# Three blocks of 43 rows instead of four of 32 in the triangular solve of a gated DeltaNet layer, and other work at the kernel's start and end

## The chip, the cores and the metric

The kernel runs on one core of a Trainium2 chip. The core has five engines that each follow their own list of instructions: TensorE (PE, products), VectorE (DVE), ScalarE (ACT), GpSimd (POOL) and SyncE (SP), which here only issues DMAs. A loading of weights into the array is recorded apart, as PEld. Counted is the device time of one execution in microseconds. Three runs took 2796.86, 2797.15 and 2800.05 us, the median is 2797.15.

## The reference

256 tokens of width 2048 pass through two layers, all in f32. Layer 0 mixes tokens with a gated DeltaNet, layer 1 with a sparse attention; behind each mixer stand a layer norm, a gated feed-forward part with a short convolution (width 5120), another layer norm, and `x + sigmoid(x Wg) * (p Wp)`. The change is in layer 0 and in the very last sigmoid product. Of layer 0 this matters:

```python
def gated_delta_rule(q, k, v, g, beta):        # 32 heads of 128, q and k shared by two
    gc = jnp.cumsum(g, axis=-1)
    kb = k * beta[..., None]
    vb = v * beta[..., None]
    ...
    decay = jnp.where(tri, jnp.exp(jnp.where(tri, diff, 0.0)), 0.0)
    lmat = jnp.where(strict, jnp.einsum('bhncd,bhnsd->bhncs', kb, k) * decay, 0.0)
    amat = lmat + jnp.eye(C, dtype=jnp.float32)
    rhs = jnp.concatenate([vb, kb * jnp.exp(gc)[..., None]], axis=-1)
    sol = lax.linalg.triangular_solve(amat, rhs, left_side=True, lower=True, unit_diagonal=True)
```

`proj = x @ w_in` gives q, k, v, a gate z and the decays; q, k and v go through a causal convolution of four taps and a silu. The kernel cuts the 256 tokens into two halves of 128 (called a = 0 and 1), so each head needs the solution of two unit lower triangular systems of 128 rows, and the second one's right side depends on the first's solution.

## The kernel before

**Products.** Nearly all of the time goes into products with the weights in f32 precision. `weights()` (L101) fetches a raw tile of 512 KB (128 x 1024 f32) on SP's queue (L109), ScalarE rounds it into a high part `hi` (L114), and VectorE makes the rest `lo` (L115). Four raw tiles and three pairs of hi and lo exist. x stands transposed on chip as xT, also as a high and a low part. `gemm_t_steps` then makes 8 products of 128 x 512 with hi (L147: both parts of x at once) and 8 of 128 x 256 with lo (L151) per tile; `gemm_steps` does it with x as the stationary side (L184, L187, L190). In `gemm_steps` the last tile is done for one half of the tokens and then for the other, so that the first half's result can be used earlier.

**Groups.** Layer 0's 32 heads go by 8 groups of 4. For a group, `keys(g)` makes k and q (8 tiles, with convolution), `zgate` the gate z (8 tiles), `values` v (8 tiles, with convolution). The loop in `gdn_groups` writes them down as: values(g), then keys(g+1) and zgate(g+1), then `inverses`, `front(g+1)`, `substitute(g+1)`, `solve(g)`, `outputs(g)`. A scheduler turns this into one list per engine, by order of writing and by priorities; every engine and every DMA queue then works strictly in order.

**The solve.** A 128 x 128 triangular matrix is treated by blocks of rows on its diagonal, here four of 32:

- `front(g)`: `sums` makes the Gram products k k' on PE (g_ps, L542 and L543), `blocks` scales them into the strictly lower matrix L on VectorE (L574), SP stores the 32 x 32 diagonal blocks (lt, 4 DMAs, L579) and loads them again so that each partition of the chip has one whole block in a row (ld, 4 DMAs, L583).
- `substitute(g)`, on POOL: all 32 blocks of a group (2 halves, 4 heads, 4 blocks) are inverted at once by forward substitution. Block and column group share the 128 partitions: 32 blocks times 4 groups of columns, with 8 columns each. The start value xi (the identity) is copied from a constant, then come 31 steps of a multiply (L612) and a subtract (L614), each one step of a chain. At its end POOL stores xi (tt, 4 DMAs, L617).
- `inverses(g)`: POOL fetches the inverted blocks onto the diagonal of pm (4 DMAs, L631; pm is otherwise zero, and there is one pm). PE multiplies them with L (w_ps, through the helper `mul`, L623: four f32 products of 128 columns or fewer, one per head), and ScalarE copies what is above the block diagonal of the product into W.
- `solve(g)`: per half y0 = pm times the right side (s_ps<-vt,pm), then three times y = y0 - W y, a product on PE (s_ps<-y,W) and a subtract on VectorE (L691). With four blocks W is nilpotent of order four, so three rounds are exact. Between the halves stands the coupling product n21.

**POOL's queue** holds, in this order: pm fetches of group g, the substitution of group g+1 with its stores, and so on. **SP's queue** holds the weight tiles in the order in which PE uses them, with lt, ld and the decays' rows between them.

**The start.** `load(nb)` fetches four blocks of 512 columns of x (two DMAs each); PE transposes each (t_ps, 8 products by the identity, L231), and ScalarE and VectorE split it into xT (L224, L225). The first weight tiles stand between the blocks on SP's queue. Behind the transposes of block 1 POOL fetches the convolution's taps (128 KB) and a table of constants, cst (448 KB).

**The end.** `ple` makes the last product by blocks of 512 columns; for each half of a block ScalarE takes the sigmoid (L899), VectorE multiplies and adds (L900, L901), and SP stores the result (L903).

## Time and profile before

| What | us |
|---|---|
| median of the three runs | 2797.15 |
| the profiled execution | 2797.12 |
| its span, first to last instruction | 2795.1 |
| group loop of layer 0, one group to the next (stretch 138.8 to 224.2) | 85.4 |
| PE busy in that stretch | 85.35 |
| DVE, ACT, POOL busy in that stretch | 66.5, 48.7, 32.6 |
| first 30 us: PE busy | 22.4 |
| last 6.1 us: PE busy | 0.7 |

The granted clock of TensorE reads 1.00 in all stretches but the last. A table of stretches gives each engine's busy time in that stretch. A timeline row has the start, the duration, the engine, the line, the operation with output and inputs, the sizes, a count where equal rows were joined, and in brackets how long the engine stood idle before it and what ended that; SPq and POOL's DMA rows are the issuing of a DMA, not its transfer. A product's row of PE says "f32" also where the operands are the rounded parts. The profile's rows of products with f32 operands count each product twice, so x8 stands for four.

### The profile page before, as it was taken

Reading aid. Unit: us, or ns where it says so; the run is one execution under the profiler, and the core shown is the slowest. Engines: PE = TensorE matmul, PEld = TensorE weight load, DVE = VectorE, ACT = ScalarE, POOL = GpSimd, SP = SyncE. Lnnn points to the kernel's source line nnn. Section 1 sums busy time; section 2 is a strip of 40 time slices with the busy share of each in tenths; the row PEclk is TensorE's granted clock in tenths of the full one; section 3 lists DMA queues with packets and bytes.
Section 4 is the critical chain, followed back from the end, with each engine's and each line's share of the span. In section 5 each row is a group of like instructions: output and inputs, shape, how many; then the busy total and the mean of one; then the engine's idle time right before and its main releaser. Section 6 shows DMA issues by size and latency. Waiting matters only on the chain. (4 is left out here: it accounts for less than half of the span.)

```text
span 2795.1 us, 40216 instructions
## 1 busy us (share of the span) xinstructions
PE 2776.6 (99%) x14958; PEld 2390.1 (86%) x14958; DVE 1856.2 (66%) x3059; ACT 1421.6 (51%) x2239; POOL 337.7 (12%) x688
## 2 busy tenths in 40 slices
PE   8999999999999999999999999999999999999999
PEld 7888888888888888888888889888888888888887
DVE  6787787877556666666545665776676666655566
ACT  4555566555445555555434544455465555543453
POOL 1543234442200000000000000120000000000000
PEclk9999999999999999999999999999999999999999
DMA  7755665655565666666556567655556666665655
GB/s 213 205 157 158 166 176 164 168 152 159 173 210 164 193 206 206 207 196 207 196 191 208 171 198 215 181 152 163 181 181 196 197 187 199 194 195 195 207 171 195
DMA packets 412275, 520.82 MB, mean 186 GB/s; under 512 B 28940, under 2 KB 301712, under 8 KB 411824
## 3 DMA queue, kind: packets, MB, share of 16 engines
q1 hardware_dynamic: 404912, 499.91, 58.9%
q0 software_dynamic: 7168, 18.35, 2.7%
q8 instruction: 117, 1.92, 0.3%
q14 instruction: 78, 0.64, 0.1%
HBM read 513.94 MB, written 7.39 MB: 187 GB/s over the span
## 5 line engine op out<-in xcount | busy, mean ns | idle before, releaser
L115 DVE TENSOR_TENSOR lo<-raw,hi 128x1024 fp32r<-128x1024 f32 (+1 forms) x921 | 1125.0, 1223 | 606.0 <-ACT hi L114 594.6
L114 ACT ACTIVATE hi<-raw 128x1024 fp32r<-128x1024 f32 (+1 forms) x921 | 967.9, 1053 | 698.9 <-PE b_ps L187 469.5
L147 PE MATMUL mm_ps<-xT,hi 128*128 128x512 f32 (+1 forms) x4176 | 1027.9, 394 | 2.6 <-ACT hi L114 2.3
L147 PEld LDWEIGHTS mm_ps<-xT,hi 128*128 128x128 f32 (+1 forms) x4176 | 762.0, 188 | 148.9 <-ACT hi L114 2.9
L151 PEld LDWEIGHTS mm_ps<-xT,lo 128*128 128x128 f32 (+1 forms) x4176 | 539.4, 191 | 22.7 <-DVE lo L115 1.5
L151 PE MATMUL mm_ps<-xT,lo 128*128 128x256 f32 (+1 forms) x4176 | 557.2, 284 | 0.4 <-DVE lo L115 0.4
L184 PE MATMUL b_ps<-hi,xT 128*128 128x512 f32 (+1 forms) x704 | 270.9, 386 | 0.0
L187 PE MATMUL b_ps<-hi,xT 128*128 128x512 f32 (+1 forms) x704 | 268.8, 383 | 0.0
L220 ACT ACTIVATE fold<-mm_ps 128x256 f32<-128x256 f32 x261 | 98.1, 376 | 268.1 <-PE mm_ps L147 267.8
L184 PE MATMUL b_ps<-hi,hTA 128*128 128x512 f32 x512 | 199.3, 389 | 0.0
L187 PE MATMUL b_ps<-hi,hTA 128*128 128x512 f32 x512 | 199.2, 389 | 0.0
L190 PE MATMUL b_ps<-lo,xT 128*128 128x512 f32 (+1 forms) x704 | 188.4, 383 | 0.0
L239 POOL DMA_DIRECT2D lng<-in_ln_g x16 | 8.8, 547 | 1239.1 <-PE b_ps L190 654.5
L612 POOL TENSOR_TENSOR xt<-ld,xi 128x60 f32<-128x60 f32 (+24 forms) x248 | 116.2, 468 | 345.1 <-DMA ld<-lt 326.3
L187 PEld LDWEIGHTS b_ps<-hi,xT 128*128 128x128 f32 x704 | 132.2, 188 | 24.8
L184 PEld LDWEIGHTS b_ps<-hi,xT 128*128 128x128 f32 x704 | 132.2, 188 | 24.1
L190 PEld LDWEIGHTS b_ps<-lo,xT 128*128 128x128 f32 x704 | 129.9, 188 | 24.5
L190 PE MATMUL b_ps<-lo,hTA 128*128 128x512 f32 x512 | 136.8, 389 | 0.0
L190 PEld LDWEIGHTS b_ps<-lo,hTA 128*128 128x128 f32 x512 | 96.1, 188 | 20.0
L184 PEld LDWEIGHTS b_ps<-hi,hTA 128*128 128x128 f32 x512 | 96.1, 188 | 20.0
L187 PEld LDWEIGHTS b_ps<-hi,hTA 128*128 128x128 f32 x512 | 96.1, 188 | 19.9
L614 POOL TENSOR_TENSOR xi<-xi,xt 128x60 f32<-128x60 f32 (+24 forms) x248 | 107.5, 433 | 19.4
(266 smaller groups left out, 2571.0 us busy)
## 6 DMA issues: line engine op xcount, KB each, us to landing
raw<-in_gdn_w_in SPq DMA_DIRECT2D x193, 512.0 KB, 4.4
raw<-in_ffn_w_gate SPq DMA_DIRECT2D x160, 512.0 KB, 4.4
raw<-in_ffn_w_up SPq DMA_DIRECT2D x160, 512.0 KB, 4.6
raw<-in_ffn_w_down SPq DMA_DIRECT2D x160, 512.0 KB, 4.1
raw<-in_dsa_w_in SPq DMA_DIRECT2D x72, 512.0 KB, 3.7
raw<-in_gdn_w_o SPq DMA_DIRECT2D x64, 512.0 KB, 4.0
raw<-in_ple_w_gate SPq DMA_DIRECT2D x64, 512.0 KB, 4.9
raw<-in_dsa_w_o SPq DMA_DIRECT2D x32, 512.0 KB, 3.9
```

Source lines behind the costliest of these rows:

```text
L114: act = nc.scalar.activation(hi, raw, AF.Copy)
L115: ins = nc.vector.tensor_tensor(lo, raw, hi.bitcast(F32), op=ALU.subtract)
L147: ins = nc.tensor.matmul(q[:m, :], hi[:, k, o:o + m], x[:, k0 + k].rearrange("p a b -> p (a b)"), start=k0 + k == 0, stop=last)
L151: ins = nc.tensor.matmul(q[:m, S:], lo[:, k, o:o + m], x[:, k0 + k, 0, :], start=False, stop=last)
L184: ins = nc.tensor.matmul(ps[a][:, :n], xh, hi, start=k == 0, stop=False)
L187: self.before = nc.tensor.matmul(ps[a][:, :n], xl, hi, start=False, stop=False)
L190: self.last = nc.tensor.matmul(ps[a][:, :n], x(k)[:, 0, a * P:(a + 1) * P], lo, start=False, stop=k == kt - 1)
L220: nc.scalar.activation(t[:m], ps[:, S:], AF.Copy)
L239: ins = self.nc.gpsimd.dma_start(out=r, in_=bass.AP(tensor=src.tensor, offset=src.offset, ap=[[0, P], [1, n]]))
L612: nc.gpsimd.tensor_tensor(tmp[:, :m, :w], bcast(ld[:, i + 1:, i], m, 1), xi[:, :m, i:i + 1].to_broadcast([P, m, w]), op=ALU.mult)
L614: nc.gpsimd.tensor_tensor(xi[:, :m, i + 1:], xi[:, :m, i + 1:], tmp[:, :m, :w], op=ALU.subtract)
```

## The change

It has four parts.

1. **The solve by 43 rows.** The blocks are rows 0 to 41, 42 to 84 and 85 to 127 (42, 43 and 43 rows): three instead of four. `solve` does two rounds instead of three. The 24 blocks of a group still take 32 of the four times 32 places on the partitions, with 12 columns each. `substitute` has 42 steps; its start value xi is fetched by a DMA from the constants' table (264 KB, one buffer) instead of copied. ld becomes two tiles that exist once for all groups, the left 22 columns (43 x 22) and the right 21 (21 x 21); storing and loading them takes 6 + 8 DMAs (L634, L638) instead of 4 + 4. pm is fetched by 3 DMAs, w_ps has 86 columns, and W is copied in 2 pieces per half.
2. **Order around it.** `front(g+1)` without its last part is called behind the first tile of zgate(g+1) instead of behind `inverses(g)`, L gets two buffers, and the parts that need q (causal, squares, mixes) move into `values`. In group 0, front(1) and seven of the eight tiles of values(1) are called ahead of inverses(0).
3. **The start.** 13 products that nobody reads (idle_ps, on zeros in a part of xT that is written later) stand on PE ahead of and behind the first transposes. Block 0's transposes are split by pairs of columns (`begin`), the first weight tile is fetched and split by halves, a second weight tile is fetched ahead of block 1, the taps are fetched behind block 2, and the constants (now 256 KB without xi's start value) and ng behind block 3. The table of ones is a memset.
4. **The end.** The last block of 512 columns is done in three turns over its last two tiles: the second half's columns 0 to 255, the first half's all 512, the second half's columns 256 to 511; sigmoid, multiply, add and store follow by these pieces.

The diff, cut to its core:

```diff
+B_ROWS, B_COLS, B_LEFT = 43, 12, 22
+B_FROM = (0, 42, 85, P)
+N_CONST = C_XINIT + B_COLS * B_ROWS
...
+        parts = (slice(0, 2), slice(2, 4)) if self.fresh else (slice(0, nk),)
...
+            turns = [((0, 1), 0, n)] if not last else [((0,), 0, n), ((1,), 0, n)]
+            if last and fine:
+                turns = [((1,), 0, n // 2), turns[0], ((1,), n // 2, n // 2)]
...
+    def warm(self, n):
+
+        ps = self.mm.tile([P, 512], F32, tag="mm", name="idle_ps")
+        x = self.xT[:, KT - 1].rearrange("p a b -> p (a b)")
+        for _ in range(n):
+            self.nc.tensor.matmul(ps, x[:, :P], x, start=True, stop=True)
+
+    def begin(self, xT, x):
+
+        nc, out = self.nc, []
+        for k in (0, 2):
+            for a in range(2):
+                ps = self.sp.tile([P, 2, P], F32, tag="bk" if k else "sp", name="t_ps")
+                for j in (k, k + 1):
+                    self.turned = nc.tensor.transpose(ps[:, j - k], x[:, a, j * P:(j + 1) * P], self.ident)
+                out.append(self.split(xT[:, k:k + 2, 0, a * P:(a + 1) * P], xT[:, k:k + 2, 1, a * P:(a + 1) * P],
+                                      ps))
+        return [out[1], out[3]]
...
+                if nb:
+                    for a in range(2):
+                        self.halves = self.to_xT(self.xT, xs[nb][:, a], a, nb * 4, to)
+                    self.halves = [self.halves]
+                else:
+                    nc.vector.memset(self.xT[:, KT - 1].bitcast(F32), 0.0)
+                    self.warm(8)
+                    self.halves = self.begin(self.xT, xs[0])
+                    self.warm(5)
...
+                         2: [(cr, t["gdn_conv_w"].rearrange("k (n c) -> n k c", c=P))],
+                         3: [(self.cst, t["cst"][:, P:C_XINIT]),
                              (ng, t["gdn_norm_g"].rearrange("(p o) -> p o", o=1))]}.get(nb, ())
...
+        lds, nl = [], B_ROWS - B_LEFT
+        for k, n, o, tall in ((B_ROWS, B_LEFT, 0, 48), (nl, nl, B_LEFT, 32)):
+            lead = B_FROM[2] + o + tall - P
+            lt = self.dr.tile([32, lead + tall, n], F32, tag=f"lt{n}", name="lt", bufs=1)
+            ld = pool.tile([P, k, n], F32, tag=f"ld{n}", name="ld")
+            nc.gpsimd.memset(ld, 0.0)
+            nc.gpsimd.dma_start(out=lt[24:, lead:lead + k], in_=ld[:8])
+            lds.append((lt, ld, k, n, o, tall, lead))
...
+                    if not nb:
+                        self.early(w_in, 0, 4, (0, 256))
...
-            lt = self.dr.tile([8, 4, 32, 32], F32, tag="lt", name="lt")
-            for b in range(4):
-                nc.sync.dma_start(out=lt[:, b].rearrange("q i j -> i q j"),
-                                    in_=L[32 * b:32 * b + 32, :, :, 32 * b:32 * b + 32].rearrange("p a h j -> p (a h) j"))
-            ld = s["ld"] = pool.tile([P, 32, 32], F32, tag="ld", name="ld")
-            for e in h4:
-                nc.sync.dma_start(out=ld[32 * e:32 * e + 32], in_=bass.AP(tensor=lt.tensor, offset=lt.offset,
-                                                                          ap=[[1024, 32], [1, 1024]]))
+            for lt, ld, k, n, o, tall, lead in lds:
+                for b, r in enumerate(B_FROM[:3]):
+                    c = r + o
+                    r0 = min(c, P - tall)
+                    at = lead - c + r0
+                    nc.sync.dma_start(out=lt[8 * b:8 * b + 8, at:at + tall].rearrange("q i j -> i q j"),
+                                      in_=L[r0:r0 + tall, :, :, c:c + n].rearrange("p a h j -> p (a h) j"))
+            for lt, ld, k, n, o, tall, lead in lds:
+                for e in h4:
+                    nc.sync.dma_start(out=ld[32 * e:32 * e + 32], in_=lt[:, lead:lead + k])
...
-            ld = s["ld"]
-            xi = pool.tile([P, 8, 32], F32, tag="xi", name="xi", bufs=2)
-            tmp = pool.tile([P, 8, 32], F32, tag="xt", name="xt", bufs=2)
-            nc.gpsimd.tensor_copy(xi, self.xinit.rearrange("p (c j) -> p c j", c=8))
-            for i in range(31):
-                w, m = 31 - i, i // 4 + 1
-                nc.gpsimd.tensor_tensor(tmp[:, :m, :w], bcast(ld[:, i + 1:, i], m, 1),
-                                        xi[:, :m, i:i + 1].to_broadcast([P, m, w]), op=ALU.mult)
-                nc.gpsimd.tensor_tensor(xi[:, :m, i + 1:], xi[:, :m, i + 1:], tmp[:, :m, :w], op=ALU.subtract)
-            tt = s["tt"] = self.dr.tile([8, 4, 8, 4, 32], F32, tag="tt", name="tt")
+            ld, right = (x[1] for x in lds)
+            xi = pool.tile([P, B_COLS, B_ROWS], F32, tag="xi", name="xi")
+            nc.gpsimd.dma_start(out=xi, in_=t["cst"][:, C_XINIT:])
+            for i in range(B_ROWS - 1):
+                w, m = B_ROWS - 1 - i, i // 4 + 1
+                col = ld[:, i + 1:, i] if i < B_LEFT else right[:, i + 1 - B_LEFT:, i - B_LEFT]
+                tmp = pool.tile([P, 132], F32, tag="xt", name="xt")[:, :m * w].rearrange("p (c j) -> p c j", c=m)
+                nc.gpsimd.tensor_tensor(tmp, bcast(col, m, 1), xi[:, :m, i:i + 1].to_broadcast([P, m, w]), op=ALU.mult)
+                nc.gpsimd.tensor_tensor(xi[:, :m, i + 1:], xi[:, :m, i + 1:], tmp, op=ALU.subtract)
+            tt = s["tt"] = self.dr.tile([32, B_COLS, 4, B_ROWS], F32, tag="tt", name="tt")
             for e in range(4):
-                nc.gpsimd.dma_start(out=tt[:, :, :, e].rearrange("q b c j -> (q b) c j"), in_=xi[32 * e:32 * e + 32])
+                nc.gpsimd.dma_start(out=tt[:, :, e], in_=xi[32 * e:32 * e + 32])
...
+            tt, rows = s["tt"], 4 * B_COLS
+            for b, r in enumerate(B_FROM[:3]):
+                r0, w = min(r, P - rows), B_FROM[b + 1] - r
+                nc.gpsimd.dma_start(out=pm[r0:r0 + rows, :, r:r + w],
+                                    in_=bass.AP(tensor=tt.tensor, offset=tt.offset + (8 * b * rows - r + r0) * B_ROWS,
+                                                ap=[[B_ROWS, rows], [rows * B_ROWS, 8], [1, w]]))
+            r1, r2 = B_FROM[1:3]
+            for a in range(2):
+                ps = self.sp.tile([P, 4, P - r1], F32, tag="bk", name="w_ps")
+                mul(s["L"][:, a], pm[:, 4 * a:4 * a + 4, r1:], ps)
+
+                for r, n in ((r1, r2 - r1), (r2, P - r2)):
+                    nc.scalar.activation(W[:r, a, :, r:r + n], ps[:r, :, r - r1:r - r1 + n], AF.Copy)
...
+                causal(s)
                 substitute(s)
+            else:
+                causal(s)
+                if g > 1:
+                    for _ in range(3):
+                        next(steps)
+                squares(s)
+                next(steps)
+                mixes(s)
...
-                for i in range(3):
+                for i in range(2):
                     ps = mul(W[:, a], y)
-                    y = u[:, a] if i == 2 else pool.tile([P, 4, P], F32, tag="y", name="y", bufs=2)
+                    y = u[:, a] if i else pool.tile([P, 4, P], F32, tag="y", name="y", bufs=2)
...
-                zgate(n, [])
+                zgate(n, [], (lambda: front(n)) if g else None)
+                if not g:
+                    front(n)
+                    for _, _ in zip(range(7), begin(n)[0]):
+                        pass
             else:
                 ahead(rest)
             inverses(s)
             if g < 7:
-                front(n)
-                mixes(n)
                 substitute(n)
             solve(s)
...
+            steps = [self.gemm_steps(t["ple_w_gate"][i], nb * 512, 512, lambda k: self.xT[:, k], KT, done(nb),
+                                     **dict(end=2, fine=True) if nb == 3 and out is not None else {})
```

**PE's list from the first w_ps of group 0 on.** g_ps is the Gram product, mm_ps the products of the next group's values, s_ps the solve. Before:

```order
L623 MATMUL w_ps<-pm,L 128x96 x8
L542 MATMUL g_ps<-k 128x256
L543 MATMUL g_ps<-k 128x128
L542 MATMUL g_ps<-k 128x256
L543 MATMUL g_ps<-k 128x128
L623 MATMUL s_ps<-vt,pm 128x128 x4
L147 MATMUL mm_ps<-xT,hi 128x512 x8
L151 MATMUL mm_ps<-xT,lo 128x256 x16
```

Now:

```order
L594 MATMUL g_ps<-k 128x256
L595 MATMUL g_ps<-k 128x128
L594 MATMUL g_ps<-k 128x256
L595 MATMUL g_ps<-k 128x128
L149 MATMUL mm_ps<-xT,hi 128x512 x8
L153 MATMUL mm_ps<-xT,lo 128x256 x16
L149 MATMUL mm_ps<-xT,hi 128x512 x16
L153 MATMUL mm_ps<-xT,lo 128x256 x16
L149 MATMUL mm_ps<-xT,hi 128x512 x16
L153 MATMUL mm_ps<-xT,lo 128x256 x16
L149 MATMUL mm_ps<-xT,hi 128x512 x16
L153 MATMUL mm_ps<-xT,lo 128x256 x8
L679 MATMUL w_ps<-pm,L 128x86 x8
L679 MATMUL s_ps<-vt,pm 128x128 x4
```

The Gram products of group 1 and 56 products of each size moved from behind the first w_ps to ahead of it.

**SP's list where the L of group 2 is gathered** (lt is the store, ld the load, raw the weight tiles; 128x4x256 are tiles of keys and values). Before:

```order
L109 DMA raw<-in_gdn_w_in 128x4x256 x10
L579 DMA lt<-L 32x8x32 x4
L109 DMA raw<-in_gdn_w_in 128x4x256
L583 DMA ld<-lt 32x1024 x4
L109 DMA raw<-in_gdn_w_in 128x4x256 x3
```

Now:

```order
L109 DMA raw<-in_gdn_w_in 128x4x256 x4
L634 DMA lt<-L 48x8x22 x3
L634 DMA lt<-L 32x8x21 x3
L109 DMA raw<-in_gdn_w_in 128x4x256
L638 DMA ld<-lt 32x946 x4
L638 DMA ld<-lt 32x441 x4
L109 DMA raw<-in_gdn_w_in 128x4x256 x4
```

The gather has 14 DMAs where there were 8, and stands behind four tiles of that kind instead of ten.

**PE's list at the start** (t_ps are transposes of x, mm_ps the products of the first tiles). Before:

```order
L231 MATMUL t_ps<-ident,x_in 128x128 x8
L147 MATMUL mm_ps<-xT,hi 128x512 x8
L151 MATMUL mm_ps<-xT,lo 128x256 x8
L231 MATMUL t_ps<-ident,x_in 128x128 x8
L147 MATMUL mm_ps<-xT,hi 128x512 x8
```

Now:

```order
L249 MATMUL idle_ps<-xT 128x512 x8
L258 MATMUL t_ps<-ident,x_in 128x128 x8
L249 MATMUL idle_ps<-xT 128x512 x5
L149 MATMUL mm_ps<-xT,hi 128x512 x8
L153 MATMUL mm_ps<-xT,lo 128x256 x8
L239 MATMUL t_ps<-ident,x_in 128x128 x8
```

Thirteen unread products were added around the first transposes; the order of the rest is the same.

More of the change, by code (lines that the diff above doesn't have):

```diff
@@ L41, in constants @@
     c[:, C_CMIN:C_CMIN + P] = np.where(j <= i, np.float32(3.4e38), np.float32(-BIG))
-    x = np.zeros((4, 32, 8, 32), np.float32)
-    for cg in range(4):
-        for k in range(8):
-            x[cg, :, k, 4 * k + cg] = 1.0
-    c[:, C_XINIT:C_XINIT + 256] = x.reshape(P, 256)
-    c[:, C_ONES:C_ONES + P] = 1.0
+    x = np.zeros((4, 32, B_COLS, B_ROWS), np.float32)
+    for n in range(B_ROWS):
+        x[n % 4, :, n // 4, n] = 1.0
+    c[:, C_XINIT:] = x.reshape(P, B_COLS * B_ROWS)
     c[:, C_CAUSAL:C_CAUSAL + P] = j <= i
@@ L89, in __init__ @@
         self.xT = self.xtp.tile([P, KT, 2, S], F32R, tag="xT", name="xT")
-        self.first, self.ready = (), {}
+        self.first, self.ready, self.fresh = (), {}, True
     def after(self, ins, to, sync=False):
@@ L158, in gemm_t_steps, with gemm_steps @@
             yield
-    def gemm_steps(self, src, c0, n, x, kt, done, also=(), end=1, held=None, pin=False):
+    def gemm_steps(self, src, c0, n, x, kt, done, also=(), end=1, held=None, pin=False, fine=False):
         nc = self.nc
@@ L179, in gemm_steps @@
             behind = self.last if last and (pin or held is not None) else None
-            for halves in ((0,), (1,)) if last else (range(2),):
+            turns = [((0, 1), 0, n)] if not last else [((0,), 0, n), ((1,), 0, n)]
+            if last and fine:
+                turns = [((1,), 0, n // 2), turns[0], ((1,), n // 2, n // 2)]
+            for halves, o, m in turns:
+                cs = slice(o, o + m)
                 for k, hi, lo in parts:
@@ L373, in gdn_gates @@
         self.gemm_t(t["gdn_w_in"], 12288, 64, self.xT, done)
-        self.after(nc.scalar.activation(al, al, AF.Exp), self.halves[0])
+        self.after(nc.scalar.activation(al, al, AF.Exp), self.halves[-1][0])
         yield
@@ L407, in gdn_gates @@
         nc.tensor.matmul(pc[:, 0:64], self.tri, g64, start=True, stop=True)
-        nc.tensor.matmul(pc[:, 64:96], self.ones, g[:, 0], start=True, stop=True)
+        ones = pool.tile([P, P], F32, tag="y0", name="ones")
+        nc.gpsimd.memset(ones, 1.0)
+        nc.tensor.matmul(pc[:, 64:96], ones, g[:, 0], start=True, stop=True)
         nc.tensor.matmul(pc[:64, 128:256], g64, self.tri, start=True, stop=True)
@@ L527, in keys @@
                         taps(self.tail)
-                    self.first = self.halves
+                    self.first = list(self.halves)
                     next(steps[0])
+                    if not nb:
+                        self.early(w_in, 0, 4, (0, 256))
                 next(steps[1])
@@ L671, in zgate @@
             for j, _ in enumerate(self.gemm_steps(w_in, 8192 + 512 * s["g"], 512, lambda k: self.xT[:, k], KT, done)):
-                if j > 2 and rest:
+                if behind is not None and not j:
+                    behind()
+                if j > 3 and rest:
                     rest.pop(0)()
```

98 lines of the change are left out of this document (50 added, 48 removed).

## The prediction

> **What bounds the kernel now.** I read the page first, then the waits of TensorE (PE), then the stretches where it isn't simply streaming: the first 30 us, the group loop of layer 0, and the last 6 us.
>
> ```profile
> PE 2776.6 (99%) x14958; PEld 2390.1 (86%) x14958; DVE 1856.2 (66%) x3059; ACT 1421.6 (51%) x2239; POOL 337.7 (12%) x688
> ```
> ```profile
> PE t_ps L231 <- DMA x_in<-in_x: 5.1, 1, 5.1
> PE mm_ps L147 <- ACT hi L114: 2.3, 2, 1.8
> ```
>
> PE is busy for 2776.6 of 2795.1 us. Of the 18.5 us that are left, 5.1 are the fetch of x, 2.3 are two waits for the first splits, and about 5 lie behind the last product. So the time falls almost exactly by what PE no longer has to issue, and rises by every new wait of PE. Nothing that another engine saves counts by itself. The profiled execution took 2797.12 us, 0.03 below the median of the runs, so the sum is made on either.
>
> **The solve, on PE.** A solve step is four f32 products of 128x128, each recorded twice. This is a stretch of PE's timeline in the second group, with the first row of the timeline behind w_ps too:
>
> ```profile
> L623 PE MATMUL s_ps<-y,W 128*128 128x128 f32 x384 | 53.9, 283 | 0.4
> ```
> ```profile
> 224.16 1.92 PE L623 MATMUL w_ps<-pm,L 128*128 128x96 f32 x16
> 225.91 0.62 PE L542 MATMUL g_ps<-k 128*128 128x256 f32 x2
> ...
> 245.36 1.15 PE L623 MATMUL s_ps<-y,W 128*128 128x128 f32 x8
> 246.27 1.20 PE L151 MATMUL mm_ps<-xT,lo 128*128 128x256 f32 x8
> ```
>
> 384 records are 48 steps: three in each of two halves of eight groups. With three blocks of rows instead of four, two steps are enough, so 16 steps go. A step holds PE from 245.36 to 246.27, 0.91 us: 16 x 0.91 = **14.6 us**. The 53.9 us of the group overlap their neighbours, so 53.9 / 48 = 1.12 would be too much (17.9 in all, the upper bound); the step before it in that stretch starts 0.81 us ahead of its follower (13.0, the lower). The product w_ps shrinks from 96 to 86 columns, but its 16 records take 225.91 - 224.16 = 1.75 us, 0.109 each, no less than a 128-column record (0.91 / 8 = 0.114). I take zero.
>
> **What it costs GpSimd (POOL), and when PE needs it.** The substitution on POOL goes from 31 to 42 steps, 62 to 84 instructions, and the mean size from 50 to 87 elements per partition (the sum over i of (rows left) x (i // 4 + 1)).
>
> ```profile
> 89.23 0.78 POOL L612 TENSOR_TENSOR xt<-ld,xi 128x31 f32<-128x31 f32 x1 [25.91 <-DMA ld<-lt]
> ...
> 125.81 2.35 POOL L617 DMA_DIRECT2D tt<-xi  x4 [0.30 <-POOL xi L614]
> 131.87 2.33 POOL L631 DMA_DIRECT2D pm<-tt  x4 [3.71 <-DMA tt<-xi]
> ...
> 164.98 0.26 POOL L612 TENSOR_TENSOR xt<-ld,xi 128x31 f32<-128x31 f32 x1 [29.72 <-DMA ld<-lt]
> ...
> 166.48 0.25 POOL L612 TENSOR_TENSOR xt<-ld,xi 128x29 f32<-128x29 f32 x1
> ...
> 175.88 0.35 POOL L612 TENSOR_TENSOR xt<-ld,xi 128x76 f32<-128x76 f32 x1
> ...
> 197.46 2.32 POOL L617 DMA_DIRECT2D tt<-xi  x4 [0.29 <-POOL xi L614]
> 202.42 2.33 POOL L631 DMA_DIRECT2D pm<-tt  x4 [2.64 <-PE mm_ps L147]
> ```
> ```profile
> L623 PE MATMUL w_ps<-pm,L x128: 245/275/275, 138.8 to 728.2; 128*128 128x96 f32 x128
> ...
> DMA to landing us min/median/max: 3.2/4.7/6.6
> ```
>
> (The last row is that of the pm fetches, L631.) Start to start an instruction took (125.8 - 89.2) / 62 = 0.59 us in group 0 and (197.5 - 165.0) / 62 = 0.52 in group 1. From 29 to 76 elements an undisturbed one grows from 0.25 to 0.35, 2.1 ns per element; 37 more are 0.08, and since the whole runs a third slower than its undisturbed rows I add 0.10. That gives 84 x 0.69 = 58 us in group 0 and 84 x 0.62 = 52 after that. The lower bound adds nothing for size (50 and 44), the upper lets an instruction grow in proportion to its elements (0.59 x 87 / 50 = 1.02, 86 us).
>
> The change pays for this with time. In group 0 it moves the Gram products of group 1 and seven of eight tiles of its value GEMM ahead of w_ps: 56 products at 0.228 and 56 at 0.119 are 19.4 us, the Gram products 1.3. With 1.1 us won at the start (below), w_ps of group 0 comes due at 138.8 + 19.4 + 1.3 - 1.1 = 158.4. The answer comes at 88.1 (the start, 1.1 sooner) + 58 + 6.1 (from the first tt issue to the first pm issue, 131.87 - 125.81) + 1.2 (two more pm issues) + 4.7 (landing) = 158.1. So it lands just as it is needed: 0 to 2 us of wait. In group 1 POOL must also fetch its start value xi, which before was a copy: issued near 154, landing 5 to 7 us later, so it begins near 161, and 161 + 52 + 5.0 + 1.2 + 4.7 = 224 against a due time of 224.2 + 1.3 - 1.8 - 1.1 = 222.6. That is 1 to 2 us. From group 2 on, the Gram products stand one z GEMM (eight tiles of 2.7 us) ahead of where they stood; a chain of 12 (Gram to lt) + 12 (to the first POOL instruction) + 52 + 11 = 87 us has 103 us, and I expect no wait. **Loss: 2.5 us**, bounds 0 and far up (the first rival).
>
> **SP's queue.** The gather of L is now six stores and eight loads, where it was four and four:
>
> ```profile
> 238.53 2.02 SPq L579 DMA_DIRECT2D lt<-L  x4
> 243.65 0.39 SPq L109 DMA_DIRECT2D raw<-in_gdn_w_in  x1
> 244.28 1.70 SPq L583 DMA_DIRECT2D ld<-lt  x4
> 246.87 10.98 SPq L109 DMA_DIRECT2D raw<-in_gdn_w_in  x3
> ```
>
> From the first store to the second weight tile behind it SP spent 246.87 - 238.53 = 8.3 us. Six more issues at 0.43 make it near 11 us. Weights are queued behind, and the loads now also wait for POOL to be done with the one ld buffer. Four raw tiles and two split ones lie ahead of PE, 6 x 2.7 = 16 us; 11 + 4 of landing + 2.3 of split is 17. It was spent beside slow solves before and is spent beside the dense z GEMM now, which is why I keep 0 to 2 us per group as a rival and take zero: the f32 products of the following value step stretch the 16 us by about 2.7.
>
> **The start.**
>
> ```profile
> 5.14 1.94 PE L231 MATMUL t_ps<-ident,x_in 128*128 128x128 f32 x8 [5.14 <-DMA x_in<-in_x]
> ...
> 8.83 3.64 PE L147 MATMUL mm_ps<-xT,hi 128*128 128x512 f32 x8 [1.75 <-ACT hi L114]
> ...
> 12.30 1.12 PE L151 MATMUL mm_ps<-xT,lo 128*128 128x256 f32 x8
> ...
> 23.41 1.06 ACT L114 ACTIVATE hi<-raw 128x1024 fp32r<-128x1024 f32 x1 [0.60 <-DMA raw<-in_gdn_w_in]
> ...
> 24.52 0.50 PE L147 MATMUL mm_ps<-xT,hi 128*128 128x512 f32 x1 [0.55 <-ACT hi L114]
> ```
> ```profile
> GB/s 0 84 218 246 311 217 317 365 372 351 304 346 362 377 368 240 258 342 341 152 171 258 212 221 5 0 110 365 332 350 128 277 183 284 83 0 45 322 97 287
> ...
> cst<-in_cst POOLq DMA_DIRECT2D x1, 448.0 KB, 7.1
> ```
>
> The first eight products took 12.30 - 8.83 = 3.47 us, 0.43 each, against 0.228 later, and PE stood 1.75 us before them. 13 products that nobody reads fill the fetch of x, and splitting by halves lets the first product start near 7. That is up to 1.75 + 1.65 = 3.4 us. But the second row shows the queues full (each figure a slice of 1.25 us): 6.8 MB in the first 23.75 us. The product at 24.52 waited for a tile that landed at 23.41, behind x, the weights ahead of it and the 448 KB of constants. A faster PE doesn't bring that tile. What brings it is less traffic: the 448 KB and the 128 KB of conv weights go later, 264 KB of xi and some 45 KB of zeros come in early, net 0.27 MB at about 0.31 MB per us, 0.9 us, plus part of the 0.55 that PE waited. I take **1.1 us**, bounds 0.3 and 3.4.
>
> **The end.** The last column block is cut so that only 256 columns of one half are left behind PE:
>
> ```profile
> 2789.11 0.61 PE L190 MATMUL b_ps<-lo,xT 128*128 128x512 f32 x2
> 2789.76 0.60 ACT L899 ACTIVATE sg<-b_ps 128x512 f32<-128x512 f32 x1 [0.76 <-PE b_ps L190]
> ...
> 2791.12 0.69 DVE L901 TENSOR_TENSOR x<-x,sg 128x512 f32<-128x512 f32 x1
> ```
>
> VectorE ends at 2791.8, 2.1 us behind PE's last product. With halves, the other half's two VectorE operations (1.4 us) begin 0.65 us behind their sigmoid and end 0.7 us behind PE; two of half size follow, to 1.45: 0.65 less, and the last store is half as long, about 0.3. Cutting 12 products of 512 into 24 of 256 costs 12 x (2 x 0.119 - 0.228) = 0.12 each way round, 0.2 in all. **0.7 us** less; bounds 0 and 1.2.
>
> The sum: 2797.1 - 14.6 - 1.1 - 0.7 + 2.5 = **2783.2 us**, rounded to 2783.
>
> **Rivals.**
>
> *POOL becomes the bound (slower).* If an instruction grows in proportion to its elements, a substitution takes 86 us in group 0 and 76 later. Then w_ps of group 0 waits 28 us, and every later group needs 76 + 11 + 6 (xi) = 93 us against a PE period near 84: 7 x 9 = 63 more. 2797 - 16 + 91 = 2872. For it: a substitution runs slower than its undisturbed rows already, and chains in groups 0 and 1 have no slack, so from 0.76 us per instruction their two waits eat the 16 us and the change is slower. Against it: 0.35 against 0.25 for 2.6 times the elements. 12 in 100, of which 7 end slower, 3 within 0.2% and 2 faster.
>
> *SP starves the weights.* 1.5 us in each of seven groups: 2783 + 10 = 2793, half of it within 0.2% of before. For it: 17 against 16 us above. Against: VectorE, relieved of 16 subtractions, may have L ready sooner. 13 in 100.
>
> *The start pays in full.* 3.4 instead of 1.1, and no wait for POOL: 2797.1 - 14.6 - 3.4 - 0.7 = 2778.4. For it: the queue lag at 23.41 (the tile was the sixth weight tile) may shrink when its issue, which waits for a split, comes sooner. Against: the full row of GB/s. 15 in 100. [...]
>
> The forecast itself, with waits of a few us, has 60 in 100. About 0.2%, 5.6 us, is what a measurement of this kernel can tell from no change. Faster by that: 60 + 15 + 8 + 2 = 85; within it 5 + 3 = 8; slower 7. The range runs from 2777, the full start with 0.91 to 1.0 us per step, to 2793, where SP or POOL costs some 10 us more.
>
> **What would show it.** In the profile after: s_ps<-y,W at 256 records; the first w_ps near 158 and the second near 223 with single-digit waits for pm; POOL's instructions at 0.6 to 0.7 us start to start; the first read product near 7 but the third stage's tile still landing past 22; PE busy near 2765. I am wrong if POOL's instructions take over 0.75 us, if PE waits for a split of weights in the middle of a group, or if the products that are left in a solve step drift apart because less work lies between them.

## The result, and the profile after

The changed kernel is slower: 2820.16 us (median, 2818.32 to 2822.26) against 2797.2 before, a ratio of 1.008 with an interval of 1.0063 to 1.0097. The forecast was 2783, with a range of 2777 to 2793. The profiled execution was the slowest of the four; it has a span of 2820.5 us, 25.4 more than before.

The page's first part, and then the waits of TensorE (engine, line, what it waited for: us in total, times, longest):

```profile
PE 2773.9 (98%) x14855; PEld 2387.6 (85%) x14855; DVE 1876.7 (67%) x3049; ACT 1428.4 (51%) x2259; POOL 482.3 (17%) x861
```
```profile
PE w_ps L679 <- DMA pm<-tt: 19.8, 2, 13.9
PE g_ps L595 <- ACT vt L735: 13.6, 6, 2.5
PE b_ps L190 <- DVE pd L229: 1.9, 2, 1.6
...
PE mm_ps L149 <- ACT hi L116: 0.7, 1, 0.7
```

PE is 2.7 us less busy, though 16 solve steps are gone, and it waits some 33 us in two new places: for pm, and for a copy of the values on ScalarE. Of the first, 13.9 us stand in group 0, where I had put 0 to 2, and 5.8 in group 7, where I had put none. The second stands in no line of the prediction.

The first w_ps, and what GpSimd and SP did for it:

```profile
170.70 3.68 PE L679 MATMUL w_ps<-pm,L 128*128 128x86 f32 x16 [13.93 <-DMA pm<-tt]
174.17 1.98 PE L679 MATMUL s_ps<-vt,pm 128*128 128x128 f32 x8
...
240.10 1.91 PE L679 MATMUL w_ps<-pm,L 128*128 128x86 f32 x16
241.81 0.71 PE L149 MATMUL mm_ps<-xT,hi 128*128 128x512 f32 x2
```
```profile
78.11 3.80 SPq L634 DMA_DIRECT2D lt<-L  x6
...
86.66 5.31 SPq L638 DMA_DIRECT2D ld<-lt  x8
...
148.88 3.39 SPq L634 DMA_DIRECT2D lt<-L  x6
```
```profile
92.11 0.27 POOL L669 TENSOR_TENSOR xt<-ld,xi 128x42 f32<-128x42 f32 x1 [31.09 <-DMA ld<-lt]
...
149.81 2.50 POOL L673 DMA_DIRECT2D tt<-xi  x4 [0.37 <-POOL xi L670]
163.75 1.91 POOL L689 DMA_DIRECT2D pm<-tt  x3 [11.44 <-DMA tt<-xi]
```

The substitution itself takes 149.8 - 92.1 = 57.7 us, 0.687 per instruction. Around it everything is later: it starts at 92.1, the tt stores take 13.9 us until pm can be fetched, and pm lands at 170.7, where PE was ready at 156.8 (170.70 - 13.93). Behind the wait the 16 records of w_ps take 174.17 - 170.70 = 3.47 us, in the next group 241.81 - 240.10 = 1.71.

Stores by size (KB each, median us from issue to landing), before and then after:

```profile
lt<-L SPq DMA_DIRECT2D x32, 32.0 KB, 4.3
tt<-xi POOLq DMA_DIRECT2D x32, 32.0 KB, 2.6
```
```profile
lt<-L SPq DMA_DIRECT2D x24, 33.0 KB, 7.5
tt<-xi POOLq DMA_DIRECT2D x32, 64.5 KB, 6.6
```

The six lt stores move pieces of 22 or 21 numbers (88 and 84 bytes) where the four before moved 32 (128 bytes): 1920 pieces instead of 1024. tt moves 1536 of 172 bytes instead of 1024 of 128.

The start and the end. The gates' product (128*64) is the first thing that both kernels do behind the start; before, it began at 37.25:

```profile
8.26 2.02 PE L149 MATMUL mm_ps<-xT,hi 128*128 128x512 f32 x8
10.11 1.12 PE L153 MATMUL mm_ps<-xT,lo 128*128 128x256 f32 x8
...
21.45 1.06 ACT L116 ACTIVATE hi<-raw 128x1024 fp32r<-128x1024 f32 x1 [0.74 <-DMA raw<-in_gdn_w_in]
...
35.28 3.83 PE L149 MATMUL mm_ps<-xT,hi 128*64 128x512 f32 x16
...
2815.24 0.64 PE L198 MATMUL b_ps<-lo,xT 128*128 128x256 f32 x4
```

The first read products run at 0.23 us each, the third stage's tile lands at 21.45 (before: 23.41), and 2.0 us are won at 35 us. PE ends at 2815.88 and the span at 2820.5, 4.6 later; before, it was 5.4. That is 0.8 less.

### The profile page after: what moved, and what is told of

It is laid out like the page before. It is cut to its first block, busy times and chain, and to the rows that moved or that the text cites. A ratio compares the mean times of both kernels' runs of the same rounds, so it can differ in the third digit from the quotient of the medians.

```text
span 2820.5 us, 40314 instructions
## 1 busy us (share of the span) xinstructions
PE 2773.9 (98%) x14855; PEld 2387.6 (85%) x14855; DVE 1876.7 (67%) x3049; ACT 1428.4 (51%) x2259; POOL 482.3 (17%) x861
## 5 line engine op out<-in xcount | busy, mean ns | idle before, releaser
L117 DVE TENSOR_TENSOR lo<-raw,hi 128x1024 fp32r<-128x1024 f32 (+2 forms) x922 | 1133.1, 1230 | 608.9 <-ACT hi L116 596.6
L116 ACT ACTIVATE hi<-raw 128x1024 fp32r<-128x1024 f32 (+2 forms) x922 | 968.0, 1052 | 712.9 <-PE b_ps L194 482.4
L190 PE MATMUL b_ps<-hi,xT 128*128 128x512 f32 (+2 forms) x708 | 273.9, 389 | 0.0
L194 PE MATMUL b_ps<-hi,xT 128*128 128x512 f32 (+2 forms) x708 | 270.9, 384 | 0.0
L669 POOL TENSOR_TENSOR xt<-ld,xi 128x120 f32<-128x120 f32 (+5 forms) x336 | 189.6, 564 | 185.4 <-DMA ld<-lt 153.4
L198 PE MATMUL b_ps<-lo,xT 128*128 128x512 f32 (+2 forms) x708 | 189.3, 384 | 0.0
L670 POOL TENSOR_TENSOR xi<-xi,xt 128x120 f32<-128x120 f32 (+5 forms) x336 | 179.3, 534 | 26.4
```

The source lines that it names most:

```text
L116: act = nc.scalar.activation(hi[:, ks], raw[:, ks], AF.Copy)
L117: ins = nc.vector.tensor_tensor(lo[:, ks], raw[:, ks], hi[:, ks].bitcast(F32), op=ALU.subtract)
L190: ins = nc.tensor.matmul(ps[a][:, cs], xh, hi[:, cs], start=k == 0, stop=False, skip_group_check=o > 0)
L194: self.before = nc.tensor.matmul(ps[a][:, cs], xl, hi[:, cs], start=False, stop=False, skip_group_check=o > 0)
L198: self.last = nc.tensor.matmul(ps[a][:, cs], x(k)[:, 0, a * P:(a + 1) * P], lo[:, cs], start=False, stop=k == kt - 1, skip_group_check=o > 0)
L669: nc.gpsimd.tensor_tensor(tmp, bcast(col, m, 1), xi[:, :m, i:i + 1].to_broadcast([P, m, w]), op=ALU.mult)
```

## The experiments

The kernel before was timed beside every set; its medians lie between 2797.7 and 2798.1.

**The price of a solve step.** In the kernel before, the third round is left out:

```diff
-                for i in range(3):
+                for i in range(2):
                     ps = mul(W[:, a], y)
```

> The kernel before, with its blocks of 32 rows, but with two rounds of y = y0 - W y instead of three: the third round, and with it the last block row's exact solution, is left out, and nothing else changes. It is the price of a step by itself. By the 0.91 us between a step's first product and the next product on PE: 2797.1 - 16 x 0.91 = 2782.5. By its busy time in the groups of instructions (1.12): 2779. If the steps' other work (values' products) loses its place beside VectorE's subtracts and PE waits instead: 2786 to 2790.

Measured: 2778.07 us, ratio 0.9928 (0.9913 to 0.9942), 19.6 us less; the bare price of a step by its busy time is what came true. The first w_ps of two groups in a row (timeline):

```profile
221.50 1.92 PE L623 MATMUL w_ps<-pm,L 128*128 128x96 f32 x16
...
304.55 1.92 PE L623 MATMUL w_ps<-pm,L 128*128 128x96 f32 x16
```

A group takes 83.05 us; before, it took 309.48 - 224.16 = 85.32. Two steps are worth 2.27, 1.14 each, 18.2 in all. Of the other 1.4 us, 0.4 stand ahead of the first w_ps (138.44 for 138.80) and 0.6 are a shorter wait of b_ps (0.8 before, 0.2 here). The 0.91 us that I read off the timeline leave out what a step costs the products beside it. Counted from each product's start to the next one's, over this period of group 1, the steps themselves fall from 5.34 to 3.62 us, the value products (mm_ps), as many as before, from 46.13 to 45.68, and s_ps<-u,n from 0.91 to 0.81. A step is thus 0.86 by itself, 0.23 at the value products, and 0.05 at the product behind.

**The Gram products' wait.** Two kernels take it away in two ways. Values turned earlier:

```diff
-                    if i and rest:
+                    if (i or j > 1) and rest:
                         rest.pop(0)()
```

> The changed kernel, but the transposes of the values (v_ps) stand two weight tiles earlier, in the second half of the k GEMM and the first half of the q GEMM. Theory: in each of six groups the second Gram product waits 1.6 to 2.5 us (13.6 in all) for one of two PSUM buffers, which a transpose of the values holds until ScalarE's last vt copy; with the transposes earlier these waits go, and with them two dips of the granted clock near 305 and 565 us (about 1.6 us each): 2820 - 13.6 - 3.3 = 2803. The waits for pm in groups 0 and 7 stay (13.9 and 5.8). Rival: the Gram product is held by ScalarE's backlog of splits and convolutions whoever owns the buffer; then the waits stay and the time is 2818 to 2822.

Measured: 2803.86 us, ratio 1.0019 (1.0010 to 1.0029). Gram products later:

```diff
-                if behind is not None and not j:
+                if behind is not None and j == 2:
                     behind()
```

> The changed kernel, but the Gram products stand behind the third tile of the z GEMM instead of the first, in groups 2 to 7. Theory of the PSUM buffer: the same 13.6 us of waits and 3.3 of clock go, but the chain from L to pm starts some 3 to 5 us later against PE, so the wait for pm in group 7 grows from 5.8 to 9 to 11 us: 2806 to 2809, 3 to 6 more than with the transposes earlier. Rival, POOL's chain has room in group 7 as well: 2803, as with the transposes earlier.

Measured: 2803.34 us, ratio 1.0020 (1.0010 to 1.0030). In both the row of g_ps is gone from PE's waits, and the group takes what it takes with two rounds in the kernel before (first w_ps of two groups, with the transposes earlier):

```profile
323.68 1.91 PE L679 MATMUL w_ps<-pm,L 128*128 128x86 f32 x16
...
406.86 1.91 PE L679 MATMUL w_ps<-pm,L 128*128 128x86 f32 x16
```

83.18 against 413.40 - 327.64 = 85.76 in the changed kernel. The mechanism stands in the changed kernel's list of ScalarE, here in group 3:

```profile
304.10 0.88 ACT L735 ACTIVATE vt<-v_ps,sv 128x128 f32<-128x128 f32 x3
304.85 1.07 ACT L116 ACTIVATE hi<-raw 128x1024 fp32r<-128x1024 f32 x1
305.79 0.52 ACT L522 ACTIVATE ac<-pd,cw 128x256 f32<-128x256 f32 x1
306.19 0.38 ACT L735 ACTIVATE vt<-v_ps,sv 128x128 f32<-128x128 f32 x1
```

The two Gram products take both buffers of the pool "sp". A transpose of the values holds one until its fourth copy, and that copy stands behind a split of weights and a convolution on ScalarE. In the kernel before, a whole z GEMM lay between the two. My figure for the second kernel was too high: the wait for pm in group 7 grew from 5.8 to 7.5 us, not to 9 or more, and the two kernels are equal within their intervals. The wait of group 0, which neither edit touches, was 13.1 and 11.5 in these traces, for 13.9, and that hides part of the difference.

**The stores that collide.** Only group 0 changes:

```diff
                 if not g:
-                    front(n)
                     for _, _ in zip(range(7), begin(n)[0]):
                         pass
+                    front(n)
```

> The changed kernel, but in group 0 the Gram products of group 1 stand behind the seven value tiles, so that the stores of L of group 1 come some 20 us later and not at the same time as POOL's stores of the inverted blocks (tt). Theory of the collision: from the first tt issue to the first pm issue it takes 6 to 9 us instead of 13.9, and the wait of group 0 for pm falls from 13.9 to about 8; in exchange the substitution of group 1 begins near 184 instead of 172.5 and PE waits about 13 us for its pm, so the time is near 2830. Rival, the tt stores are slow by their own small pieces: 13 to 14 us again, a wait of 13.9 in group 0, and near 2830 to 2835.

Measured, in a single execution: 2836.82 us. The POOL rows:

```profile
148.29 2.50 POOL L673 DMA_DIRECT2D tt<-xi  x4 [0.37 <-POOL xi L670]
157.47 1.90 POOL L689 DMA_DIRECT2D pm<-tt  x3 [6.69 <-DMA tt<-xi]
...
234.91 2.47 POOL L673 DMA_DIRECT2D tt<-xi  x4 [0.29 <-POOL xi L670]
248.63 1.90 POOL L689 DMA_DIRECT2D pm<-tt  x3 [11.26 <-DMA tt<-xi]
```

tt to pm falls to 9.2 us in group 0, and its wait to 6.8. In group 1 it rises to 13.7: there SP now issues the lt stores of group 2 from 232.69 on, beside tt, and PE waits 19.8 us for pm, where I expected 13. So the collision moves with the stores, and by this run about 4.7 of the 13.9 us are its work. The rest, 9.2 against 6.1 before, is left without lt stores beside it. The transfers between 150 and 160 us, in the changed kernel and then in this one:

```profile
DMA packets 2826, 1.11 MB, mean 111 GB/s; under 512 B 2096, under 2 KB 2762, under 8 KB 2826
```
```profile
DMA packets 2054, 2.15 MB, mean 215 GB/s; under 512 B 115, under 2 KB 2000, under 8 KB 2054
```

Beside the lt stores half the bytes moved, at 111 GB/s for 215, with 2096 packets under 512 bytes for 115.

**The products behind a wait.** On the kernel with the earlier transposes, unread products fill the waits of groups 0 and 7:

```diff
+            for _ in range({0: 52, 7: 24}.get(s["g"], 0)):
+                ...
+                self.after(nc.tensor.matmul(idle, xx[:, :P], xx, start=True, stop=True), ...)
             for a in range(2):
                 ps = self.sp.tile([P, 4, P - r1], F32, tag="bk", name="w_ps")
```

> The kernel with the earlier transposes of the values, and 52 products that nobody reads ahead of the first w_ps of group 0 and 24 ahead of that of group 7, into PE's waits for pm (13.1 and 6.7 us; 52 and 24 times 0.228 are 11.9 and 5.5). If the slow products behind these waits (16 records of w_ps in 3.5 us instead of 1.75) come from PE standing idle, they run at full rate now and about 3.5 us are won at each place: 2803.9 - 7 = 2797. If they are slow for what they read, nothing changes: 2803 to 2805.

Measured: 2799.61 us, ratio 1.0010 (1.0000 to 1.0019), 4.3 less than without them, though the two intervals overlap; in the two traces it is 7.6, but the one without them is the slowest of its ten executions. The stretches 160 to 180 and 735 to 750 (busy time of PE, PEld, DVE, ACT, POOL, then granted clock, DMA share, GB/s), without and with the unread products:

```profile
160.00:180.00 20.00, 10.92 (x56) 10.19 (x56) 1.38 (x2) 1.60 (x5) 10.26 (x28) 0.58 0.57 150
...
735.00:750.00 15.00, 13.86 (x70) 12.34 (x71) 3.63 (x7) 2.66 (x6) 0.00 (x0) 0.73 0.11 33
```
```profile
160.00:180.00 20.00, 20.00 (x120) 17.18 (x119) 4.65 (x10) 3.99 (x10) 11.70 (x29) 1.00 0.61 156
735.00:750.00 15.00, 15.00 (x100) 12.89 (x100) 6.32 (x11) 4.59 (x14) 0.00 (x0) 1.00 0.25 72
```

The granted clock stays at 1.00, and w_ps behind the wait takes its 1.75 us again (168.48 to 170.23). So the products were slow for the idle time ahead of them, not for what they read; by the traces each long wait cost its own length and some 3.4 us of slow products (from the start of w_ps to that of the same product behind it 10.86 us without the unread products and 7.48 with them in group 0, 6.96 and 3.71 in group 7).

**Both ends alone**, in the kernel before: all of the change's hunks for the start and the end, with the solve and its order left at four blocks (cst keeps xi's start value, 448 KB). Its core:

```diff
+                    self.warm(8)
+                    self.halves = self.begin(self.xT, xs[0])
+                    self.warm(5)
...
+                         2: [(cr, t["gdn_conv_w"].rearrange("k (n c) -> n k c", c=P))],
+                         3: [(self.cst, t["cst"][:, P:]),
...
+                                     **dict(end=2, fine=True) if nb == 3 and out is not None else {})
```

> The kernel before with the change's start and end alone (unread products, splits by halves, constants later, last column block by pieces); the solve stays at four blocks of 32. By the trace of the changed kernel, where the gates' first product starts at 35.28 instead of 37.25 and 0.7 us are won at the end: 2797.5 - 2.0 - 0.7 = 2794.8. By the recorded sum (1.1 and 0.7): 2795.7. Rival, the start's gain is given back at the first wait behind it: 2796.5 to 2797.5.

Measured: 2795.48 us, ratio 0.9993 (0.9983 to 1.0002): between 4.8 us less and 0.6 more, not told from no change. The trace shows what becomes of the start. The gates' product begins at 34.77, 2.5 sooner than before, but:

```profile
79.51 1.02 PE L581 MATMUL g_ps<-q,k 128*128 128x256 f32 x2 [2.94 <-DVE L L613]
...
139.49 1.92 PE L662 MATMUL w_ps<-pm,L 128*128 128x96 f32 x16
```
```profile
71.30 0.40 ACT L531 ACTIVATE L<-qd,ngc 128x128 f32<-128x128 f32 x1 [3.80 <-DMA qd<-grow]
...
71.74 0.35 DVE L545 SCALAR_TENSOR_TENSOR qd<-qd,gc,cst 128x128 f32<-128x128 f32 x1 [3.23 <-ACT L L531]
```

At 80 us PE waits 2.9 for VectorE, which finishes L only 0.4 sooner than before (the Gram product had waited 0.54 there). VectorE is not what sets the pace: it had stood idle for 3.2 us behind ScalarE, and ScalarE for 3.8 until the decays' rows (qd) landed. Their DMA was issued 1.9 sooner than before, at 63.44, and landed only 0.4 sooner. The products behind PE's wait are slow (the Gram products take 2.38 us, 79.51 to 81.89, where those of the next group take 1.32, 153.73 to 155.05), and w_ps of group 0 starts at 139.49 (before: 138.80). So in this execution, whose 2797.32 us are the most of the ten, the start's gain was lost behind a transfer. The median of the ten, 2795.48, lies nearer to the sum with the gain (2795.7) than to the rival's 2796.5 to 2797.5, and the interval holds both. Whether the gain reaches the end stays open.

**The unread products alone** are taken out of the changed kernel:

```diff
-                    self.warm(8)
                     self.halves = self.begin(self.xT, xs[0])
-                    self.warm(5)
```

> The changed kernel without its 13 unread products and without the memset that they read. If they buy the full rate of the first read products, the first eight take 0.43 us each again instead of 0.23, 1.7 us in all, and the gates' first product (35.28 with them) starts near 37. If the tiles of weights hold PE at 22 us anyway, the wait there (0.69 with them) takes that up and it starts at 35.3 to 36. The rest is the changed kernel's, so 2820 to 2823.

Measured, in a single execution: 2815.63 us. The first eight products take 3.5 us again and the gates' product starts at 36.21:

```profile
7.36 3.75 PE L149 MATMUL mm_ps<-xT,hi 128*128 128x512 f32 x8 [0.60 <-ACT hi L116]
10.91 1.91 PE L153 MATMUL mm_ps<-xT,lo 128*128 128x256 f32 x8
...
168.51 3.69 PE L676 MATMUL w_ps<-pm,L 128*128 128x86 f32 x16 [11.26 <-DMA pm<-tt]
```

So they are worth about 1 us at 36 us (with them it is 34.5 to 35.3 in all kernels), and none at the first w_ps: there PE waits for GpSimd, which began at 91.9 in this kernel and at 92.1 in the changed one. PE was ready for it at 157.3 (168.51 - 11.26), 0.5 later than in the changed kernel, and pm landed 2.2 sooner, so that it waited 2.7 less. With one execution the difference of 4.5 us in the total is not a verdict.

**More work ahead of w_ps**, on the kernel with the earlier transposes:

```diff
-                zgate(n, [], (lambda: front(n)) if g else None)
+                zgate(n, [], lambda: front(n), {0: 2, 1: 1}.get(g, 0))
                 if not g:
-                    front(n)
                     for _, _ in zip(range(7), begin(n)[0]):
                         pass
+                    opening(2, 3)
+                    gather()
...
-            nc.gpsimd.dma_start(out=xi, in_=t["cst"][:, C_XINIT:])
+            nc.gpsimd.memset(flat, 0.0)
+            for e in range(4):
+                ...
+                nc.gpsimd.memset(flat[32 * e:32 * e + 32, e:e + (B_ROWS + 4) * top + 1:B_ROWS + 4], 1.0)
...
-            for j in range(6):
+            for j in range(8):
                 for g in begun:
```

(`opening(2, 3)` starts three tiles of the keys of group 2, `gather` is the ld loads.)

> The kernel with the earlier transposes of the values, and four more edits that give GpSimd's chain room. Group 0: the Gram products of group 1 stand behind the third tile of its z GEMM, so that L is stored ahead of the tt stores and not beside them, its loads stand later in SP's queue, and three tiles of the keys of group 2 are put ahead of the first w_ps. Group 1: two value tiles ahead of w_ps. Every group: xi is set by five memsets on GpSimd (1 us) and not fetched (6.9 us). Group 7: four more tiles of the output projection ahead of w_ps. Theory: the waits for pm (13.1 and 6.7 us) and the slow products behind them (3.5 us each) go and nothing replaces them: 2803.9 - 13.1 - 6.7 - 7 = 2777. Rival: the earlier loads block SP, or the transposes wait for VectorE, and half of it is given back: 2785 to 2795.

Measured: 2789.5 us, ratio 0.9969 (0.9958 to 0.9981). It is faster than the kernel before and than the changed one. Against the kernel with the earlier transposes 14.4 us came of the 26.8 that were expected. The wait of group 7 is gone; in group 0 pm still lands late:

```profile
169.54 3.69 PE L707 MATMUL w_ps<-pm,L 128*128 128x86 f32 x16 [3.57 <-DMA pm<-tt]
```

tt to pm took 160.8 - 149.9 = 10.9 us there: the lt stores are out of its way, but SP's loads of L are not. Three further orders of the same work gave no more. All eight value tiles ahead (besides this line, the transposes in group 1 and the Gram product behind them stand one to two tiles later):

```diff
-                    for _, _ in zip(range(7), begin(n)[0]):
+                    for _, _ in zip(range(8), begin(n)[0]):
```

> The kernel with more work ahead of w_ps, but in group 0 all eight value tiles and three tiles of keys stand ahead of it (eleven instead of ten), and in group 1 the transposes of the output and the values stand one to two tiles later, as does the Gram product behind them. Theory: the wait of group 0 for pm (3.6) and the products at half rate behind it (3.5) go, and so does the wait of a transpose for VectorE (2.9): 2789.5 - 7 - 2.9 = 2779.6. Rival: pm lands later again, because the loads of L of group 1 run beside the tt stores; then a wait of 1 to 3 us with its slow products is left: 2783 to 2787.

Measured: 2789.29 us, ratio 0.9965 (0.9951 to 0.9978). PE no longer waits for pm, but 4.1 us for ScalarE, whose copies of W now stand behind the convolution of the eighth value tile:

```profile
174.23 0.42 ACT L526 ACTIVATE v<-ac 128x256 f32<-128x256 f32 x1 [2.56 <-DVE ac L524]
...
176.75 0.88 ACT L730 ACTIVATE W<-w_ps 42x172 f32<-42x172 f32 x4
```

Back to seven, with the loads of L of group 1 on GpSimd's queue (and three value tiles instead of two ahead of w_ps in group 1):

```diff
-                    gather()
+                    gather(nc.gpsimd)
```

> The kernel with eleven tiles ahead, taken back to ten (seven value tiles and three of keys), but with the loads of L of group 1 on GpSimd's own queue behind its pm fetch instead of on SP's, and three instead of two value tiles ahead of the w_ps of group 1. Theory: the tt stores of group 0 now run beside weight tiles only, so that tt to pm takes 8 to 9 us and not 11 to 13, pm lands at 164 before w_ps is due at 166, no products run at half rate behind it, and SP is not held: 2789.3 - 7 = 2782. The substitution of group 1 begins 4 us later, so its pm may cost 1 to 2 us. Rival, tt is slow beside the weight tiles as well: a wait of 2 to 4 us and the half rate stay, 2788 to 2790.

Measured: 2793.31 us, ratio 0.9983 (0.9974 to 0.9992). tt to pm is 10.6 us with weight tiles alone beside it, so the rival was right on that point. The wait of group 0 fell to 1.6, and slow products still followed it:

```profile
169.34 1.84 PE L711 MATMUL s_ps<-vt,pm 128*128 128x128 f32 x8
170.83 1.63 PE L153 MATMUL mm_ps<-xT,lo 128*128 128x256 f32 x6
```

From its first product to the next one behind it this step takes 1.49 us, where 0.81 is undisturbed (179.03 to 179.84), and the granted clock reads 0.95 from 169 to 240, a stretch that also holds a wait of 3.4 at a transpose (ot_ps). In group 1, whose substitution began at 173, a wait of 4.1 came back, with slow products too (w_ps takes 3.47 us, 242.18 to 245.65).

The loads on SP again, with unread products ahead of w_ps (and the transposes behind the solve of group 0 one tile later):

```diff
+            for _ in range(0 if s["g"] else 14):
+                ...
+                self.after(nc.tensor.matmul(idle, xx[:, :P], xx, start=True, stop=True), self.tail)
```

> The kernel with ten tiles ahead of w_ps in group 0 (its loads of L of group 1 on SP again, two value tiles ahead in group 1), with 14 unread products (3.2 us) in what is left of the wait for pm in group 0 (3.6), and with the transposes behind the solve of group 0 one tile later. If the half rate behind the wait is all that idle time costs beside itself, 3.5 us of it go, and 1 to 3 us of the transpose's wait for VectorE (2.9): 2789.4 - 3.5 - 2 = 2784. If pm lands later in this order too, 2787 to 2789.

Measured: 2789.17 us, ratio 0.9965 (0.9954 to 0.9977). The clock between 169 and 240 us is at 1.00 (0.93 without the 14 products), but w_ps starts at 172.26 instead of 169.54: a late split (1.3 us of wait) brought the tiles ahead of it to their end at 169.05, 3 us later than without, and the unread products then stood in the way. The transpose's wait of 2.9 did not move. The three orders at 2789 us are equal within their intervals.

## Why the prediction was wrong, point by point

**What bounds the kernel: right.** The time followed PE's work and its waits. 25.4 us of span are made up of: 18.2 less for the solve, 2.0 for the start, 0.8 for the end; 19.8 more for pm, 13.6 for the Gram products, 1.1 for one more wait of b_ps (1.9 for 0.8). That leaves 11.9 (25.4 + 21.0 - 34.5). Slow products behind the two waits for pm are 3.5 each, and two of the waits for the Gram products have some 1.6 us of slow products behind them, 10.2 together; 1.7 stays unexplained.

**The solve: right in direction, mis-sized.** 14.6 us were taken, 17.9 stood as the upper bound, and 18.2 is what two rounds instead of three are worth. What I wanted to take off as overlap is paid by the products next to a step, 0.28 us each. That error was in the change's favour.

**POOL's time per instruction: right.** 57.7 us against 58 in group 0, and 222.0 - 172.5 = 49.5 against 52 in group 1. The first rival, instructions that grow with their elements, did not happen (0.69 us, its break-even was 0.76). Yet the outcome it gave, chains in the first groups without slack, is what came.

**The step that failed** is the path around the substitution: the answer at 88.1 + 58 + 6.1 + 1.2 + 4.7 = 158.1. Measured: 92.1 + 57.7 + 13.9 + 1.3 + 5.7 = 170.7. I carried two transfer times over from a trace in which the pieces were 128 bytes and no other small stores ran beside them.

- From L to the first POOL instruction: the stores' issue 3.8 us, their landing 86.66 - 81.91 = 4.75, the loads 5.45; 14.0 in all, where it was 9.2 before (80.04 to 89.23). I charged the six more DMAs to SP's queue and to the weights, and nothing to this chain. L itself was 1.9 sooner (78.11 for 80.04).
- From tt to pm: 13.9 for 6.1. Of the 7.8 more, 3.3 to 4.7 go away without small pieces of L beside tt (10.6 and 9.2 us in two orders). I put the other 3.1 to 4.5 down to the larger stores, 64.5 KB for 32; no run changes their size alone, so that part is argued. The change moves the lt stores of group 1 ahead, to 148.88, and tt begins at 149.81. SP's order showed them moved, and I asked only what they do to the weights.

**The wait that was not there: "I expect no wait" from group 2 on.** The Gram products stand a z GEMM earlier, and I asked only whether POOL's answer has time. I did not ask what buffer they need. "Where a stall goes" has two sides: who waits for the moved work, and what the moved work now waits for. Group 7 was missed too: I gave it the cover of a full period, but with no keys and no z GEMM behind it, PE reached w_ps(7) 92.5 us after the second Gram product, and the chain took 98.4, where my sum had 87.

**SP starves the weights: did not happen** in the changed kernel; PE's waits for a split are 1.2 us in all.

**The start: the gain of 2.0 at 35 us lies inside the bounds**, above the 1.1 taken. The third stage's tile landed at 21.45, not past 22. The upper bound of 3.4 counted the first eight read products at 0.228 us behind unread ones, an estimate that no trace of before shows; they took 1.85 us (8.26 to 10.11), and 3.55 (7.36 to 10.91) where the unread ones were left out. PE's own gain was lost in the wait for pm, so adding it to the sum was not safe: the first w_ps waits for GpSimd's chain, and the trace of before had a first sign of a limit ahead of it, the Gram product's 0.54 us behind L at 79.91. How much of the gain came through that chain no run tells. **The end: 0.8** for 0.7.

**What a wait costs: missing.** Each wait was counted at its length. The slow products behind it add 3.5 us to each of the two long ones, and 1.6 to two of the six short ones.

The signs that were named: s_ps<-y,W at 256 records came true, and POOL's 0.59 to 0.69 us nearly so. The third stage's tile came before 22, the first read product at 8.26 for 7, the first w_ps at 170.7 for 158, with a wait of two digits, and the second at 240.1 for 223. PE is 2773.9 busy for 2765, mainly as slow products, the 10.2 us above, count at their length. Two conditions under which I called myself wrong, POOL over 0.75 us and waits for weights, did not come: the copy of the values stood in no sign.

## What to carry to other kernels

When work moves to an earlier place, list for it what it needs there (here two buffers that ScalarE had to free, 13.6 us of waits), not only who waits for it. Do not carry a transfer's time over when its size, its pieces or what runs beside it change, above all into a chain without slack: tt to pm took 6.1 us with pieces of 128 bytes, and with pieces of 172 bytes 13.9 beside the lt stores, 10.6 beside weight tiles alone and 9.2 without lt stores in another order. And a gain ahead of another engine's limit may be no gain: look where the first wait behind it stands before you add it to a sum. Here 2.0 us were won at 35 us, and PE then waited 13.9 for pm.

## What the runs showed of the hardware

A wait can cost more than its length, and not always. Both of these follow the same wait of the changed kernel, in groups 3 and 4:

```profile
306.62 0.71 PE L595 MATMUL g_ps<-k 128*128 128x128 f32 x4 [2.46 <-ACT vt L735]
...
307.48 0.63 PE L190 MATMUL b_ps<-hi,xT 128*128 128x512 f32 x1
307.91 0.63 PE L194 MATMUL b_ps<-hi,xT 128*128 128x512 f32 x1
...
393.99 0.71 PE L595 MATMUL g_ps<-k 128*128 128x128 f32 x4 [2.41 <-ACT vt L735]
...
394.77 0.39 PE L190 MATMUL b_ps<-hi,xT 128*128 128x512 f32 x1
395.00 0.39 PE L194 MATMUL b_ps<-hi,xT 128*128 128x512 f32 x1
```

Behind the first, products start 0.43 us apart from 307.48 to 310.04, and the granted clock reads 0.87 from 300 to 310; behind the second they start 0.23 apart at a clock of 1.00 (390 to 400). Two of six such waits were followed by slow products (the other at 565.44, with a clock of 0.84 from 560 to 570), and so was each wait of 3.57 to 19.81 us at w_ps and in the solve that a timeline here shows. Among the shorter ones, length alone does not tell the two cases apart. A wait of 2.91 us for the same transposes (ot_ps) in group 0 was followed by products that start 0.43 us apart in the kernel with more work ahead (208.58 to 209.86), and by none that are slow in the last one, with 14 unread products (0.23 apart from 207.72 on). From 169 to 240 us, w_ps included, the granted clock reads 0.93 and 1.00. The wait of 1.6 us at w_ps above was followed by slow ones too (1.49 us for a step of 0.81).
